# Right operands of the w_mo product: prepared ahead and kept in DRAM, instead of summed and split where they are used

## The chip, the cores and the metric

One core of a Trainium2 chip runs the whole program. The metric is device time in microseconds. Engines: TensorE (PE) multiplies, VectorE (DVE), ScalarE (ACT) and GpSimd (POOL) work on elements, and the sync queue (SP) issues nearly all transfers.

## The reference

One decoder layer on 1024 tokens of width 1024, in float32:

```python
x = x + hybrid_mixer(rmsnorm(x, norm_mix), w_in, ..., w_out)
x = x + memory_attention(rmsnorm(x, norm_mem), rmsnorm(mem, norm_memkv), w_mq, w_mkv, w_mo)
x = x + conv_ffn(rmsnorm(x, norm_ffn), w_up, conv_w, conv_b, w_down)
return rmsnorm(x, norm_final)
```

The mixer has one input projection, three kinds of attention (differential, dilated, and one that keeps the top 256 keys of each query) and an output projection. `memory_attention` is `softmax(q k^T / 16) v` over 256 memory tokens in four heads, with `q = h @ w_mq`, and its result `o` of 1024 x 1024 goes through `o @ w_mo`, which is the product that the change concerns.

## The kernel before, in words

**Precision.** Every float32 matrix is split in a high part (a copy by ScalarE to the type fp32r) and a low part (the source minus the high part, by VectorE or GpSimd). `mm3` (L182) multiplies high by high, high by low and low by high: three matmuls of 128 x 128 by 128 x 512 for one step.

**Strassen products.** The products with w_out (`prod_a`), w_mq (`prod_b`) and w_mo (`prod_d`, L1931) are of 1024 x 1024 by 1024 x 1024, done with seven products of half size in place of eight (`class Product`, L1390). Each of the seven, called n, has four chunks c of 128 along the inner dimension; such a pair is a unit, and it has an order x, from 0 to 83 (56 to 83 for `prod_d`). A unit needs one left and one right operand of 128 x 512, each a pair of high and low. Where the method wants a sum, it is made first, in place of one of the raw blocks (`left_of`, `right_of` L1374, `operand` L1385): the right operands of n = 1, 2 and 3 are raw blocks of w_mo, those of 5, 6, 7 and 4 are sums, 16 units in all. A unit of `prod_d` takes two of eight slots, so it begins when the unit four before it has been multiplied. Product 4, the last, walks over its four chunks twice, each time for two of the four row blocks. In `prod_d` the left operands come from the attention's output Q, the right ones from w_mo, loaded raw into two tiles `wraw` by `load_weights` (L1623) when `prod_b` has all its operands (`tiles_d` L1901), and `needs_d` (L1923) makes units wait for these loads.

**Order of the work.** The order of the instructions on PE, ACT and DVE (and POOL in the second part) is fixed before the program is built, by a model: `class Flow` runs generators that yield an engine, a cost and a rank, and each modelled engine takes the lowest rank in its queue. Engines and the sync queue then carry their instructions out in the order of emission, each waiting for its own data. `ready` (L105) chooses between DVE and POOL for operations that may go to either (`either`, L1313), by the longer of the engine's queue and the queue of a shared port, plus the cost; `issue` (L117) makes such an operation wait until the port is free. There are two flows: the mixer (`build_mixer`, L304) and everything up to the first eight products of the up-projection. In the mixer the attention's items have ranks 0 to 63, the evacuations of the projections -1, the projections on PE 100, and the top-k search 200 or, when it is late, -4.

**After the product.** The sums of `prod_d` are added to the rows of the residual stream (`x1rows`). Rows 0 to 3 (of eight blocks of 128) are complete after product 3, the fifth of the order 1, 5, 6, 2, 3, 7, 4. `normed_rows` (L1531) squares them on ACT, takes the root on DVE in twelve small steps, and scales them on DVE (`xn<-x1rows`, rank 83.2 for rows 0 to 3, 82 for the others); `turned_rows` (L1555) transposes them on PE into the tiles h3T. From these the up-projection's operands T1 to T7 are made (`half_operand` L2353, `tokens` L2386): T1 and T2 are splits of rows 0 to 3, the others hold sums that include rows 4 to 7. The up-projection begins with two products that need T1 and T2 for each of two weight columns, and then needs T7. The T tiles take the places of `prod_d`'s operands and rows; the tiles of h3T, T7 and T3 are counted in `tp_s`.

Of the kernel before, what the change touches and what calls it, by code (L numbers as in the profile page):

```python
# [14 lines left out]
F32 = mybir.dt.float32  # L15
F32R = mybir.dt.float32r
# [5 lines left out]
OP = mybir.AluOpType  # L22
AX = mybir.AxisListType

P = 128
# [24 lines left out]
class Gate:  # L50
    def __init__(self):
        self.open, self.waiting = False, []
# [7 lines left out]
class Flow:  # L60
# [3 lines left out]


    def __init__(self):
        self.t, self.events, self.count = 0.0, [], 0
        self.queue = {e: [] for e in (PE, ACT, DVE, POOL, DMA)}
        self.free = {e: True for e in self.queue}
        self.load = dict.fromkeys(self.queue, 0.0)  # L70
        self.port, self.port_load = 0.0, 0.0
# [33 lines left out]
    def ready(self, s, op):  # L105
        self.count += 1
        if isinstance(op[0], tuple):
            e = min(op[0], key=lambda e: max(self.load[e], self.port_load) + op[1][e])
            op = (e, op[1][e], partial(op[2], e), op[3], True)
        self.load[op[0]] += op[1]  # L110
        if len(op) > 4:
            self.port_load += op[1]
        rank = op[3] if len(op) > 3 else s[1]
        heapq.heappush(self.queue[op[0]], (rank, self.count, s, op))
        self.issue(op[0])

    def issue(self, e):  # L117
        if self.free[e] and self.queue[e]:
            _, _, s, op = heapq.heappop(self.queue[e])
            op[2]()  # L120
# [39 lines left out]
def trunk(ctx, tc, a, out):  # L160
# [98 lines left out]
    memk_d = [dram.tile([P, KC, MEM], F32, name=f"memk_{s}") for s in range(2)]  # L259
    memv_d = [dram.tile([P, 2, D], F32, name=f"memv_{s}") for s in range(2)]  # L260

    def gload(pool, g, tag, **kw):
# [24 lines left out]
    SMALL = 0.15  # L287
    SETUP = 26.0
    WARM = 1
    COLD = 6.0  # L290
# [13 lines left out]
    def build_mixer():  # L304
# [945 lines left out]
        def load_mixed(half, u):  # L1250
            yield mixed[u, half]
            yield from move(0.73, load(mix[half][:, u], mix_d[u][half]))

        where_w = {f"iq{c}": 3072 + P * c for c in range(4)}
        for u, cs in enumerate(units):
# [19 lines left out]
        go(late_pieces(), 80)  # L1275
        go(out_weights(), 90)
        with tc.manual_schedule(engines=engines):
            flow.run()
# [34 lines left out]
    def either(n, f, rank):  # L1313
        return (DVE, POOL), {DVE: t_dve(n), POOL: t_pool(n)}, f, rank

# [74 lines left out]
    class Product:  # L1390
# [14 lines left out]
        def unit(self, n, c):  # L1405
# [11 lines left out]
            a = go(operand(sa, x, *left_of(n, lambda i, j: self.A(i, j, c))), x)  # L1417
            b = go(operand(sb, x, *right_of(n, lambda i, j: self.B(i, j, c), self.last)), x)
            yield a
# [196 lines left out]

    h2, wm, wo2 = {}, {}, {}
    h2_in, h2_hit = after_each([(l, q) for l in range(2) for q in range(2)], 4)
    wm_in = {(j, i): Gate() for j in range(2) for i in range(2)}
    wo2_in = {(j, i): Gate() for j in range(2) for i in range(2)}  # L1620
    h2_new = {l: Gate() for l in range(2)}
# [279 lines left out]
    def tiles_d():  # L1901
        yield from all_made(prod_b, 7, 4)
        for j in range(2):
            go(load_weights(a["w_mo"][0], wo2, wo2_in, j, 56), 56)
        for _ in range(2):
            put(tp_s)
# [16 lines left out]
    def needs_d(n, c):  # L1923
        return {
            1: (o_done[c, 0], wo2_in[0, c // 2]),
            5: (o_done[c, 1], o_done[4 + c, 1]),
            6: (wo2_in[1, c // 2],),
            2: (o_done[4 + c, 0],),
        }.get(n, ())
# [4 lines left out]
        lambda i, j, c: Q[4 * j + c][:, i],  # L1934
        lambda i, j, c: wo2[i][:, c, 512 * j : 512 * j + 512],
        needs_d,
# [18 lines left out]
    def xn_slots():  # L1955
# [4 lines left out]
        for _ in range(4):  # L1960
            put(x_s)
        for _ in range(2):
            put(tp_s)

# [727 lines left out]
```

## Time and profile before

| | us |
|---|---|
| time, median of 3 runs (lowest, highest) | 1650.21 (1649.19, 1655.34) |
| the profiled execution, its own time | 1653.56 |
| its span, first to last instruction | 1651.8 |
| PE busy | 1591.3 |
| DVE busy | 1432.7 |
| ACT busy | 922.7 |
| POOL busy | 469.0 |

The stages follow each other in the trace: the mixer to about 667 us, the product with w_out, the product with w_mq from about 753, the memory attention from about 800, the product with w_mo up to 976, the up-projection from 992 to about 1424, and the down-projection. A busy time counts an instruction from its start to its end, so neighbours on a pipelined engine overlap; the starts tell the pace.

### The profile page before, as it was taken

The page shows a single profiled execution, that of the slowest core. Times are in us where ns is not written, and L with a number is a line of the kernel's source. Part 1 is how long each engine was busy: PE and PEld are TensorE (multiplying, and loading weights), DVE is VectorE, ACT ScalarE, POOL GpSimd, SP SyncE. Part 2 cuts the span into 40 slices and gives each one's busy share as a digit, 9 for nine tenths or more (in the row PEclk, how much of TensorE's full clock was granted, in tenths as well). Part 3 has the DMA queues.
Part 4 walks back from the last instruction along what each step waited for, and adds up shares of the span by engine and source line. Part 5 has one row for each costly group of instructions (what it writes and reads, how often), then busy time and mean ns, then how long its engine had stood idle before and what let it go on. Part 6 is the DMA issues. An engine that isn't in the chain of part 4 may idle for free.

```text
span 1651.8 us, 23507 instructions
## 1 busy us (share of the span) xinstructions
PE 1591.3 (96%) x7853; PEld 1319.2 (80%) x7853; DVE 1432.7 (87%) x2721; ACT 922.7 (56%) x1753; POOL 469.0 (28%) x541
## 2 busy tenths in 40 slices
PE   7989999999999999999999988999999999999997
PEld 7778888888888877878888866888888888887885
DVE  7557999999899987899988999898788888889986
ACT  5345688699865466646655455444444444453443
POOL 3311333232321103010111103342223232436672
PEclk9999999999999999999999999999999999999998
DMA  8484344523434464524052121222222221986532
GB/s 292 121 258 119 96 102 110 125 80 102 123 85 107 122 217 160 197 105 153 1 191 77 52 102 51 73 89 82 89 89 91 77 77 52 324 296 214 185 128 102
DMA packets 162619, 211.25 MB, mean 128 GB/s; under 512 B 13546, under 2 KB 101954, under 8 KB 162498
## 3 DMA queue, kind: packets, MB, share of 16 engines
q1 hardware_dynamic: 161921, 207.65, 40.2%
q10 hardware_dynamic: 576, 2.10, 0.3%
q8 instruction: 62, 1.02, 0.3%
q14 instruction: 60, 0.48, 0.1%
HBM read 145.16 MB, written 41.74 MB: 113 GB/s over the span
## 4 chain that ended last, share of the span: by engine, by line
PE 68%; DVE 19%; issue 6%; DMA 3%; POOL 2%; ACT 1%; SPq 1%; DVEq 0%; ACTq 0%; POOLq 0%
PE up L183 8%; PE up L184 8%; PE up L185 8%; PE pj L183 5%; PE pj L185 5%; PE pj L184 5%; DVE operands L1317 3%; PE trp L980 2%; DVE s L120 2%; PE pr L184 2%; PE dn L184 2%; PE dn L185 2%; PE pr L185 2%; PE dn L183 2%; PE pr L183 2%
## 5 line engine op out<-in xcount | busy, mean ns | idle before, releaser
L184 PE MATMUL up<-T,wo 128*128 128x512 f32 x616 | 242.3, 393 | 4.2 <-DVE T L1317 4.2
L183 PE MATMUL up<-T,wo 128*128 128x512 f32 x616 | 241.6, 392 | 1.5 <-ACT wo L2013 1.2
L185 PE MATMUL up<-T,wo 128*128 128x512 f32 x616 | 241.8, 393 | 0.0
L2011 POOL TENSOR_TENSOR wst<-wst 128x512 f32<-128x512 f32 x82 | 123.3, 1514 | 306.2 <-DVE wo L2005 253.9
L183 PE MATMUL pj<-h1T,wh 128*128 128x512 f32 (+1 forms) x464 | 189.4, 408 | 0.0
L185 PE MATMUL pj<-h1T,wl 128*128 128x512 f32 (+1 forms) x464 | 182.3, 393 | 0.0
L184 PE MATMUL pj<-h1T,wh 128*128 128x512 f32 (+1 forms) x464 | 182.0, 392 | 0.0
L2013 ACT ACTIVATE wo<-wst 128x512 fp32r<-128x512 f32 x144 | 89.6, 628 | 165.5 <-PE up L185 92.3
L184 PEld LDWEIGHTS up<-T,wo 128*128 128x128 f32 x616 | 116.0, 188 | 31.0 <-DVE T L1317 5.4
L183 PEld LDWEIGHTS up<-T,wo 128*128 128x128 f32 x616 | 116.0, 188 | 28.0 <-ACT wo L2013 1.6
L185 PEld LDWEIGHTS up<-T,wo 128*128 128x128 f32 x616 | 116.1, 188 | 25.8 <-DVE wo L1317 0.4
L183 PE MATMUL pr<-operands 128*128 128x512 f32 x336 | 134.6, 400 | 2.0 <-ACT operands L120 1.8
L184 PE MATMUL pr<-operands 128*128 128x512 f32 x336 | 132.8, 395 | 2.4 <-DVE operands L1317 2.2
L185 PE MATMUL pr<-operands 128*128 128x512 f32 x336 | 132.2, 394 | 2.3 <-DVE operands L1317 2.3
L120 POOL TENSOR_TENSOR wl<-st,wh 128x512 fp32r<-128x512 f32 (+1 forms) x58 | 77.5, 1336 | 192.3 <-ACT wh L120 184.9
L2005 DVE TENSOR_TENSOR wo<-wst,wo 128x512 fp32r<-128x512 f32 x141 | 118.2, 840 | 3.5 <-ACT wo L2013 3.5
L2044 DVE SCALAR_TENSOR_TENSOR ring<-ring,convv 128x1023 f32<-128x1023 f32 (+1 forms) x88 | 116.8, 1329 | 0.0
L120 ACT ACTIVATE s<-s,nm 128x128 f32<-128x128 f32 (+7 forms) x128 | 98.9, 773 | 29.1 <-DVE nm L120 26.9
L184 PE MATMUL dn<-dl,dh 128*128 128x512 f32 x280 | 109.4, 391 | 1.0 <-DVE dl L2236 0.9
L185 PE MATMUL dn<-dh,dl 128*128 128x512 f32 x280 | 109.2, 390 | 0.0
L183 PE MATMUL dn<-dh 128*128 128x512 f32 x280 | 109.0, 389 | 0.0
L185 PEld LDWEIGHTS pj<-h1T,wl 128*128 128x128 f32 (+1 forms) x464 | 86.6, 187 | 20.4
(352 smaller groups left out, 4189.2 us busy)
## 6 DMA issues: line engine op xcount, KB each, us to landing
wst<-in_w_up_dram SPq DMA_DIRECT2D x44, 512.0 KB, 3.8
st<-in_w_in_dram SPq DMA_DIRECT2D x56, 256.0 KB, 2.9
passing<-act SPq DMA_DIRECT2D x48, 256.0 KB, 3.9
act<-ring SPq DMA_DIRECT2D x22, 512.0 KB, 2.6
passing<-in_w_down_dram SPq DMA_DIRECT2D x42, 256.0 KB, 6.6
score<-in_w_mkv_dram SPq DMA_DIRECT2D x32, 256.0 KB, 4.0
kd<-kh SPq DMA_DIRECT2D x64, 128.0 KB, 2.3
kl<-kl SPq DMA_DIRECT2D x64, 128.0 KB, 2.3
```

What stands on the lines that cost most here:

```text
L120: op[2]()
L183: nc.tensor.matmul(ps, lh, rh, start=start, stop=False)
L184: nc.tensor.matmul(ps, lh, rl, start=False, stop=False)
L185: nc.tensor.matmul(ps, ll, rh, start=False, stop=stop)
L980: nc.tensor.transpose(tr[:, j * P : (j + 1) * P], s[x][:, kb * P : (kb + 1) * P], ident)
L1317: return either(n, lambda e: engine[e].tensor_tensor(out, x, y, op), rank)
L2005: eng.tensor_tensor(s[:, 1], src, s[:, 0].bitcast(F32), OP.subtract)
L2011: e.tensor_tensor(src, a, b, op)
L2013: nc.scalar.activation(s[:, 0], src, AF.Copy)
L2044: f()
```

## The change

A new generator `prepare` in the mixer, beginning at 46 us of the model's time, makes the 28 right operands of `prod_d`: in each step it loads a block of w_mo (128 x 512), makes the sum if there is one (DVE or POOL), copies the high part (ACT), makes the low part (DVE or POOL) and stores both in DRAM, all with rank 60. `prod_d` then loads each right operand ready, high and low in one transfer of 512 KB. The loads of raw w_mo, their gates and their two tiles go; the two tiles are counted free for h3T and T at once. In the model, an operation that needs the port now names the engines for which it does, and an engine whose first operation would wait for the port for more than 0.1 us takes the best one that doesn't need it.

```diff
     def ready(self, s, op):
         self.count += 1
         if isinstance(op[0], tuple):
-            e = min(op[0], key=lambda e: max(self.load[e], self.port_load) + op[1][e])
-            op = (e, op[1][e], partial(op[2], e), op[3], True)
+            e = min(op[0], key=lambda e: max(self.load[e], self.port_load if e in op[4] else 0.0) + op[1][e])
+            op = (e, op[1][e], partial(op[2], e), op[3]) + ((True,) if e in op[4] else ())
...
     def issue(self, e):
         if self.free[e] and self.queue[e]:
-            _, _, s, op = heapq.heappop(self.queue[e])
+            q = self.queue[e]
+            free = [x for x in q if len(x[3]) < 5] if self.port > self.t + 0.1 and len(q[0][3]) > 4 else []
+            _, _, s, op = x = min(free or q[:1], key=lambda x: x[:2])
+            q.remove(x)
+            heapq.heapify(q)
...
+    wmo_d = {(n, c): dram.tile([P, 2, 512], F32, name=f"wmo_{n}_{c}") for n in range(1, 8) for c in range(4)}
...
+    PREPARE = 46.0
...
+        def prepare():
+
+            yield PREPARE
+            x, y = (ip.tile([P, 512], F32, name=f"prep{i}") for i in "xy")
+            high, low = ip.tile([P, 512], F32R, name="preph"), y.bitcast(F32R)
+            both = lambda n: ((DVE, POOL), {DVE: dve(n), POOL: pool(n)})
+            eng = lambda e: nc.vector if e == DVE else nc.gpsimd
+            for c in range(4):
+                for n, dst, (i, j), diff in (
+                    (1, x, (0, 0), None), (5, y, (0, 1), (y, x)), (6, y, (1, 1), (y, x)), (4, y, (1, 0), (y, x)),
+                    (2, x, (1, 0), None), (3, x, (1, 1), None), (7, y, (0, 1), (x, y)),
+                ):
+                    r = (4 * i + c) * P
+                    yield from move(0.73, load(dst, a["w_mo"][0][r : r + P, 512 * j : 512 * j + 512]), rank=60)
+                    if diff:
+                        yield *both(512), lambda e, diff=diff: eng(e).tensor_tensor(x, *diff, OP.subtract), 60, (DVE, POOL)
+                    yield ACT, act(512, 1), partial(nc.scalar.activation, high, x, AF.Copy), 60
+                    yield *both(512), lambda e: eng(e).tensor_tensor(low, x, high.bitcast(F32), OP.subtract), 60, (DVE, POOL)
+                    yield from move(1.46, copy(wmo_d[n, c][:, 0], high), copy(wmo_d[n, c][:, 1], low), rank=60)
+                    yield 1.0
...
+        go(prepare(), 60)
...
     def either(n, f, rank):
-        return (DVE, POOL), {DVE: t_dve(n), POOL: t_pool(n)}, f, rank
+        return (DVE, POOL), {DVE: t_dve(n), POOL: t_pool(n)}, f, rank, (DVE, POOL)
...
-            b = go(operand(sb, x, *right_of(n, lambda i, j: self.B(i, j, c), self.last)), x)
+            if self.B is None:
+                b = go(moved(1.46, partial(rdma, sb, wmo_d[n, c])), x)
+            else:
+                b = go(operand(sb, x, *right_of(n, lambda i, j: self.B(i, j, c), self.last)), x)
...
     def tiles_d():
         yield from all_made(prod_b, 7, 4)
-        for j in range(2):
-            go(load_weights(a["w_mo"][0], wo2, wo2_in, j, 56), 56)
-        for _ in range(2):
+        for _ in range(4):
             put(tp_s)
...
-            1: (o_done[c, 0], wo2_in[0, c // 2]),
+            1: (o_done[c, 0],),
             5: (o_done[c, 1], o_done[4 + c, 1]),
-            6: (wo2_in[1, c // 2],),
...
-        lambda i, j, c: wo2[i][:, c, 512 * j : 512 * j + 512],
+        None,
...
         yield from all_made(prod_d, 4)
         for _ in range(4):
             put(x_s)
-        for _ in range(2):
-            put(tp_s)
```

## Rows read from the trace of the kernel before

**Rows 1.** Page, busy us (share of the span) xinstructions of each engine.

```profile
PE 1591.3 (96%) x7853; PEld 1319.2 (80%) x7853; DVE 1432.7 (87%) x2721; ACT 922.7 (56%) x1753; POOL 469.0 (28%) x541
```

**Rows 2.** Windows: length; busy PE, PEld, DVE, ACT, POOL (xinstructions); clock; DMA share; GB/s.

```profile
46.00:165.00 119.00, 110.48 (x537) 88.60 (x534) 71.40 (x120) 57.47 (x117) 21.69 (x19) 0.97 0.57 164
165.00:413.00 248.00, 246.65 (x1338) 208.95 (x1337) 236.84 (x711) 200.22 (x486) 81.51 (x224) 1.00 0.41 103
...
845.00:949.80 104.80, 103.46 (x537) 88.17 (x536) 89.53 (x161) 57.13 (x124) 11.85 (x8) 1.00 0.25 83
...
964.00:976.70 12.70, 10.06 (x36) 7.64 (x36) 10.54 (x28) 3.46 (x6) 1.84 (x1) 0.87 0.20 83
976.70:992.20 15.50, 10.58 (x64) 7.95 (x64) 15.08 (x50) 11.30 (x21) 0.00 (x0) 0.89 0.17 69
992.20:1003.00 10.80, 6.57 (x21) 4.55 (x22) 10.48 (x14) 9.97 (x17) 0.00 (x0) 0.89 0.37 98
1003.00:1024.00 21.00, 20.99 (x88) 16.48 (x87) 20.30 (x22) 9.41 (x14) 7.28 (x1) 0.97 0.00 1
```

**Rows 3.** Instructions on `wraw`, 840 to 980 us; durations min/median/max ns.

```profile
L120 ACT ACTIVATE operands<-wraw x28: 614/632/637, 848.0 to 966.6; 128x512 fp32r<-128x512 f32 x28
L1317 DVE TENSOR_TENSOR operands<-wraw,operands x27: 677/687/694, 850.3 to 967.7; 128x512 fp32r<-128x512 f32 x27
L1317 DVE TENSOR_TENSOR wraw<-wraw x15: 679/686/695, 879.7 to 965.8; 128x512 f32<-128x512 f32 x15
```

**Rows 4.** Timeline of TensorE: start, us, line, operation, count [idle before, releaser].

```profile
964.87 0.50 PE L183 MATMUL pr<-operands 128*128 128x512 f32 x1 [0.91 <-ACT operands L120]
967.11 0.79 PE L184 MATMUL pr<-operands 128*128 128x512 f32 x1 [1.74 <-DVE operands L1317]
...
970.82 0.39 PE L185 MATMUL pr<-operands 128*128 128x512 f32 x1
...
976.28 0.39 PE L185 MATMUL pr<-operands 128*128 128x512 f32 x1
...
985.86 1.06 PE L1564 MATMUL trr<-ident,xn 128*128 128x128 f32 x8 [0.71 <-DVE ry L120]
...
992.22 0.51 PE L183 MATMUL up<-T,wo 128*128 128x512 f32 x1 [0.35 <-ACT T L120]
...
1000.91 0.79 PE L184 MATMUL up<-T,wo 128*128 128x512 f32 x1 [3.95 <-DVE T L1317]
```

**Rows 5.** Timeline of VectorE, the same columns.

```profile
961.01 2.49 DVE L120 TENSOR_TENSOR v<-pr,v 128x512 f32<-128x512 f32 x4
963.40 0.69 DVE L1317 TENSOR_TENSOR wraw<-wraw 128x512 f32<-128x512 f32 x1
964.00 0.70 DVE L1317 TENSOR_TENSOR operands<-q,operands 128x512 fp32r<-128x512 f32 x1
...
976.64 1.28 DVE L120 SCALAR_TENSOR_TENSOR xn<-x1rows,ry,gb 128x1024 f32<-128x1024 f32 x1
...
989.27 2.50 DVE L1317 TENSOR_TENSOR wst<-wst 128x512 f32<-128x512 f32 x4
...
1004.38 4.63 DVE L2005 TENSOR_TENSOR T<-h3T,T 128x1536 fp32r<-128x1536 f32 x4
```

**Rows 6.** GpSimd's groups by form, 165 to 413 us: busy us, mean ns.

```profile
L120 POOL TENSOR_TENSOR wl<-st,wh 128x512 fp32r<-128x512 f32 x28 | 37.5, 1341 | 34.9 <-ACT wh L120 32.5 <-PE pss L724 2.4
```

**Rows 7.** Waits of TensorE, 46 to 125 us: total us, times, longest.

```profile
PE psi L723 <- DMA qs<-ql: 4.0, 2, 2.5
```

**Rows 8.** Page, DMA issues: count, KB each, us to landing.

```profile
wst<-in_w_up_dram SPq DMA_DIRECT2D x44, 512.0 KB, 3.8
st<-in_w_in_dram SPq DMA_DIRECT2D x56, 256.0 KB, 2.9
```

**Rows 9.** DMA issues from 845 to 960 us, the same columns.

```profile
x1rows<-x SPq DMA_DIRECT2D x8, 512.0 KB, 6.3
```

**Rows 10.** Windows of 10 us in the mixer, columns as in rows 2.

```profile
90.00:100.00 10.00, 7.49 (x33) 5.98 (x32) 4.30 (x7) 3.58 (x8) 1.30 (x1) 0.98 1.05 325
```

More of the change, by code (lines that the diff above doesn't have):

```diff
@@ L1614, in trunk @@
     )
-    h2, wm, wo2 = {}, {}, {}
+    h2, wm = {}, {}
     h2_in, h2_hit = after_each([(l, q) for l in range(2) for q in range(2)], 4)
     wm_in = {(j, i): Gate() for j in range(2) for i in range(2)}
-    wo2_in = {(j, i): Gate() for j in range(2) for i in range(2)}
     h2_new = {l: Gate() for l in range(2)}
```

## Prediction, made before the changed kernel ran

> **What bounds the kernel now.** I read the page first: TensorE is busy for 96% of the span, VectorE for 87% [rows 1]. So only a place where TensorE stands still, or runs at the lower clock, can give time back. Next I read the table of stretches and looked for such places near the code that the change touches [rows 2]. The reader should see three things in it. From 46 to 165 us TensorE has 8.5 us idle and VectorE, ScalarE and GpSimd have 47.6, 61.5 and 97.3 us. From 165 to 413 us TensorE misses 1.4 us and VectorE 11.2 us of 248, so there the mixer is full, while GpSimd still has 166 us. And between 964 and 1003 us TensorE loses 2.6, 4.9 and 4.2 us, at a granted clock of 0.87 to 0.89, while VectorE is full: 45.9 of 47.3 us from 976.7 to 1024.
>
> The third place is the end of the product with w_mo and the passage to the up-projection, and the timeline says who is late there. TensorE waits 0.91 us and 1.74 us for a w_mo operand's high and low part, then the last matmul starts at 976.28 and the first of the up-projection at 992.22; its second product stalls until 1000.91 for VectorE's low part of T [rows 4]. On VectorE the sum for a right operand of the last product starts only at 963.40, behind the four sums of product 7, and the first normalised row starts at 976.64, although its rows were complete when product 3 had been added [rows 5]. VectorE is the late one, and it is late because of the queue in front of these instructions.
>
> **What the change removes there.** In the product with w_mo it takes away 28 ScalarE copies (632 ns), 27 VectorE subtractions and 15 VectorE sums, with one of each on GpSimd [rows 3]. Back to back, VectorE starts one every 0.60 us (963.40 to 964.00) [rows 5], so 42 x 0.60 = 25 us of VectorE and some 17 us of ScalarE go, spread over 848 to 968 us. Four loads of 1 MB go too; 28 loads of 512 KB come.
>
> *Before 949.8.* TensorE misses 1.3 us of 104.8 there [rows 2]; between 0 and that can come back. I take 1.0.
>
> *964 to 1024.* This stretch takes 60.0 us. What TensorE must do in it at the higher clock: matmuls start every 0.2275 us (24 from 970.82 to 976.28), and 36 of product 4 remain at 964: 8.2 us. 64 transposes, eight in 1.06 us of which the last takes 0.27, so 0.113 each: 7.2 us. The first product of the up-projection and one matmul more, 13 x 0.2275 = 3.0 us, then 23.1 us without a stall from 1000.91 to 1024 [rows 4]. Together 41.5 us, so at most 18.5 us can be won.
>
> What is left of the waits is my choice. (a) The units of product 4 get their slots from product 7, chunk by chunk, and product 4 goes over its chunks in pairs of row blocks, so its chunk 3 is asked for when product 7 ends and needed 3 x 6 x 0.2275 = 4.1 us later. A 512 KB transfer lands 3.8 us after its issue [rows 8], 6.3 us when eight of them are sent together [rows 9]. Waiting ends between 0 and 2.5 us; I take 1.0, since nothing large is sent beside it. (b) With VectorE freed, the four normalised rows 0 to 3 can be done during product 4, and the four sums for the first up operands (989.27) as well [rows 5]; their transposes then lie inside product 4. T1 and T2 still need a tile that prod_d's operands or rows hold until then, and four copies and subtractions. I take 1.5 us. (c) T7 comes last. VectorE must still do, from about 974 us on, four sums (2.4), the small steps of three roots (3), rows 4 to 7 (4.8), the subtractions of T1 and T2 (4.8), two token sums (4.5) and T7 (2.3): 21.8 us, so 996; before, T7's low parts ran from 1004.38 to 1009 [rows 5]. TensorE has 10.9 us of products and 3.6 us of transposes to do from 976.5, so it waits some 4 us. That leaves 6.5 us of waiting: 18.5 - 6.5 = **12 us gained**. Ends: 6 us, if (b) and (c) are no better than half, and 16.
>
> **What it adds in the mixer.** 28 steps, each a load of 256 KB, a ScalarE copy (0.62), a subtraction, two stores of 256 KB, and in 16 of them a sum first. One step lasts about 2.9 us to land [rows 8], 0.63, 1.34 on GpSimd [rows 6], again 2.9 for the stores, 1.0 pause and, in 16 of 28, another 1.34: 9.5 us, an estimate from these rows. So some 12 steps run before 165 us, where the idle time above covers their 19 sums and subtractions (11 us on VectorE or 25 on GpSimd) and 8 us of ScalarE. The other 16 run in the full stretch with 25 such operations: 15 us on VectorE against 11 us idle, or 34 us on GpSimd against 166. The planner compares the queue of each engine plus the operation, so where VectorE has a queue it picks GpSimd. At rank 60 they stand behind nearly all attention work, ahead only of the top-k search when that is on time. I cost the engines at nothing; if that cover is gone, 25 x 0.60 = 15 us of attention work moves towards the mixer's end.
>
> What isn't covered is waiting in order. The planner lets the reader of a load follow 0.73 + 0.9 = 1.6 us behind it, the trace has 2.9 [rows 8], so ScalarE, VectorE or GpSimd can stand 1.3 us per step in front of everything behind it: 0 to 36 us for 28 steps. The sync queue gets 84 issues more, each ahead of a load or a copy of the attention. The nearest row is TensorE's wait for copied queries in this stretch, 4.0 us in two waits [rows 7], with 10 us of 16 full transfer engines (share 1.05) near it [rows 10]. Below nothing: a newly laid out list can also close part of the 8.5 us idle. Ends: 3 us gained, 36 lost. I take **3 us lost**, nearest to that row, since engines other than TensorE have slack in the first half of the steps.
>
> **Traffic.** The change moves 7.3 MB of loads and 14.7 MB of stores into the mixer, and 14.7 MB instead of 4.2 into the product. In the product that is 512 KB per 12 matmuls (2.7 us), while the transfer engines are busy for 0.25 of the time at 83 GB/s [rows 2] and carry 325 GB/s when full [rows 10]: 1.6 us of 2.7. I cost it at nothing beyond (a).
>
> **The other edits.** The new port rule lets a list take work without the port when the port is held. GpSimd has 8 instructions from 845 to 949.8 [rows 2], so the rule has few occasions: nothing, within 1 us either way. Two tiles more are free for h3 and T early; T waits for its source anyway: nothing.
>
> **Sum.** -12 - 1 + 3 = -10 us. The profiled execution took 1653.56 us (span 1651.8 and 1.8 around it), 3.4 above the median of 1650.21; against the median the sum gives **1640 us**.
>
> **Rivals.** *B, only half the tail.* Product 4 still waits for its last transfer, the T tiles come free only at its end, and rows 4 to 7 end late anyhow, so the chain behind them sets the end. For it: T7 and the parts after it hang on rows that product 4 completes. Against it: VectorE is full, so the queue is real. -6 - 1 + 3: 1646.
> *C, a queue that only moves.* The ranks may leave the normalised rows behind product 4's work even with VectorE free, so the gap of 16 us stays and only the stall of 2.6 us goes. Against it: VectorE ran out of such work even now, 10.54 us busy of the 12.7 before 976.7 [rows 2]. -2.6 - 1 + 3: 1649.
> *D, slower: waits in the mixer.* Every step's first reader stands at the head of its engine until the load lands. If TensorE loses the whole 1.3 us in all 28 steps, the mixer costs 36 us and the time is 1650 - 13 + 36 = 1673; at 0.8 us per step, 22 us, it is 1659. It decides from 13/28 = 0.46 us per step on. For it: the full stretch and the narrow margin. Against it: the view of rows 7 has no wait of TensorE for a load of w_in, which the same lists lay out, and GpSimd, which should get most of the sums, has few others behind it.
> *E, transfers as the bound.* 32.5 MB more, at the 325 GB/s of [rows 10], are 100 us if none of it lies beside other work: 1740. Against it: the engines are busy for 0.57 of the time at most in the stretches of [rows 2] up to 413 us and 0.25 in the product, so nearly all of it has room.
> The Trainium skill, page "SBUF — State Buffer", section "A bandwidth-pool intuition that's wrong (but worth ruling out)", says that HBM is almost always the bottleneck end to end, which speaks for E; the shares in this trace do not agree with it.
>
> **How the numbers follow.** About 0.5% (8.25 us) is what a measurement here can tell from no change: 1642.0 and 1658.5 are the bounds. Forecast 0.53, spread 1634 to 1646 by its ends; B 0.27; C 0.10; D 0.08; E 0.02. Three quarters of the forecast lie under 1642 and a fifth of B: faster 0.45. D and E lie above 1658.5: slower 0.10. The rest, 0.45, is within. The range 1632 to 1655 takes in the forecast's ends, B and C, and leaves out D, E and the extreme of the tail.
>
> **What would show it.** Right: no w_mo split in the product, VectorE with about 25 us less busy time from 845 to 976; the first normalised row ahead of product 4's end; a gap of 3 to 6 us, not 16, before the first up product; prepared operands before 350 us, mostly on GpSimd. The forecast is wrong if the first up product still comes 12 us or more behind the last of w_mo, or if the mixer ends over 8 us later, with TensorE waiting behind ScalarE or VectorE instructions that wait for a transfer.

## The result, and the profile after

The changed kernel takes **1670.16 us** (median of 4 runs, 1666.67 to 1673.41) beside 1651.24 for the kernel before on the same chip: ratio **1.0106, 95% interval 1.0079 to 1.0134**. It is slower by 1.1%, where the prediction had 1640 us and a range up to 1655. The profiled execution took 1672.66 us, 2.5 above its median.

The windows of the changed kernel, columns as in [rows 2]; the last five are the product with w_mo, its end, and the passage, some 14 to 22 us later than before.

```profile
46.00:165.00 119.00, 106.19 (x515) 84.14 (x514) 75.34 (x125) 57.45 (x118) 22.04 (x19) 0.97 0.72 221
165.00:413.00 248.00, 237.71 (x1259) 196.79 (x1258) 234.87 (x659) 192.86 (x461) 105.27 (x223) 1.00 0.55 154
866.00:971.50 105.50, 105.50 (x548) 90.23 (x547) 75.13 (x140) 46.52 (x108) 9.81 (x7) 1.00 0.59 190
985.70:998.40 12.70, 11.86 (x63) 9.27 (x62) 12.60 (x30) 5.00 (x10) 0.00 (x0) 1.00 0.38 153
998.40:1006.10 7.70, 4.34 (x28) 3.45 (x27) 7.55 (x30) 7.50 (x15) 0.00 (x0) 0.85 0.33 136
1006.10:1016.90 10.80, 10.80 (x47) 8.66 (x46) 9.78 (x21) 6.37 (x12) 0.00 (x0) 0.79 0.01 2
1016.90:1042.00 25.10, 21.55 (x81) 16.57 (x79) 21.54 (x24) 13.79 (x19) 4.41 (x1) 0.86 0.22 63
```

Beside [rows 2] the reader sees two kernels in one. In the product TensorE now misses nothing (105.50 of 105.50 us; it missed 1.3 of 104.8). In the mixer TensorE is idle for 10.3 us of the stretch from 165 to 413 us, where it was idle for 1.4, and for 12.8 from 46 to 165, where it was 8.5. VectorE, nearly as full as before (234.87 us), has 659 instructions behind it where it had 711: each takes longer, or other ones are being done.

Five marks of the two traces divide the difference: the first matmul of the product with w_out (the mixer's end), the first sum of product 7 on VectorE (961.01 in [rows 5]), the first matmul of the up-projection, the first use of its result, and the end of the span.

| mark, us | before | after | after - before |
|---|---|---|---|
| first matmul of the product with w_out | 670.2 | 695.3 | +25.1 |
| product 7 taken from PSUM | 961.01 | 981.82 | +20.8 |
| first up matmul | 992.2 | 1006.1 | +13.9 |
| first `ring<-up,ta` | 1024.4 | 1042.4 | +18.0 |
| span | 1651.8 | 1670.8 | +19.0 |

So the mixer loses 25.1 us, the products win 4.3, the passage to the first up matmul wins 6.9 more, and the start of the up-projection gives 4.1 back.

The preparation's instructions, in the view of the tile `prepx` (durations min/median/max in ns, first and last start in us; the last line is the time from a load's issue to its landing):

```profile
L125 ACT ACTIVATE preph<-prepx x28: 613/630/644, 63.1 to 430.0; 128x512 fp32r<-128x512 f32 x28
L1278 POOL TENSOR_TENSOR prepy<-prepx,preph x15: 1277/1295/1381, 199.6 to 430.7; 128x512 fp32r<-128x512 f32 x15
L1278 DVE TENSOR_TENSOR prepy<-prepx,preph x13: 670/682/693, 64.5 to 310.7; 128x512 fp32r<-128x512 f32 x13
...
L1276 POOL TENSOR_TENSOR prepx<-prepy,prepx x7: 1288/1290/1386, 186.4 to 376.5; 128x512 f32<-128x512 f32 x7
L1276 DVE TENSOR_TENSOR prepx<-prepy,prepx x5: 693/693/1743, 72.1 to 170.6; 128x512 f32<-128x512 f32 x5
L1276 DVE TENSOR_TENSOR prepx<-prepx,prepy x2: 679/685/691, 133.1 to 221.0; 128x512 f32<-128x512 f32 x2
L1276 POOL TENSOR_TENSOR prepx<-prepx,prepy x2: 1295/1296/1298, 318.4 to 423.6; 128x512 f32<-128x512 f32 x2
...
DMA to landing us min/median/max: 3.4/4.2/5.0
```

A step takes 13.6 us, not 9.5, so 9 of the 28 begin before 165 us, not 12. Of the 44 sums and subtractions 24 went to GpSimd and 20 to VectorE.

What TensorE waits for from 165 to 440 us, first before, then after (total us, times, longest):

```profile
PE av L1011 <- DVE ptl L120: 0.6, 1, 0.6
PE pss L723 <- DVE nm L120: 0.6, 1, 0.6
```

```profile
PE pss L730 <- DVE nm L125: 4.1, 4, 2.1
PE av L1018 <- DVE ptl L125: 3.3, 7, 1.1
PE trp L987 <- DVE s L125: 1.5, 3, 0.9
```

VectorE is late there, with no transfer in TensorE's list. Between 46 and 165 us it is the queries' copies again, as in [rows 7]. Two other lists of that stretch show what stands in order in front of such work: the sync queue is held at the stores until ScalarE has made the high part, and VectorE at the first reader of a step's load. Which of the two makes the copies late is not shown.

```profile
PE psi L730 <- DMA qs<-ql: 7.7, 4, 2.8
```

```profile
SPq L172 <- ACT preph L125: 13.0, 5, 4.8
```

```profile
DVE prepx L1276 <- DMA prepy<-in_w_mo_dram: 7.2, 5, 3.5
```

The passage, on TensorE and on VectorE, as in [rows 4] and [rows 5]:

```profile
988.88 0.47 PE L188 MATMUL pr<-operands 128*128 128x512 f32 x1 [0.84 <-DMA operands<-wmo]
...
993.85 0.63 PE L1596 MATMUL trr<-ident,xn 128*128 128x128 f32 x4
...
1006.14 0.78 PE L188 MATMUL up<-T,wo 128*128 128x512 f32 x1
...
1023.10 0.51 PE L188 MATMUL up<-T,wo 128*128 128x512 f32 x1 [1.79 <-ACT T L2193]
...
1024.93 0.80 PE L189 MATMUL up<-T,wo 128*128 128x512 f32 x1 [1.32 <-DVE T L2031]
```

```profile
992.42 2.48 DVE L125 SCALAR_TENSOR_TENSOR xn<-x1rows,ry,gb 128x1024 f32<-128x1024 f32 x2
...
998.41 0.69 DVE L125 TENSOR_TENSOR x1rows<-pr,x1rows 128x512 f32<-128x512 f32 x1
...
1003.21 0.69 DVE L1346 TENSOR_TENSOR T<-h3T,T 128x512 fp32r<-128x512 f32 x1
...
1011.63 1.76 DVE L2190 TENSOR_TENSOR h3T<-h3T,h3T 128x1536 f32<-128x1536 f32 x1 [0.98 <-ACT h3T L125]
1013.31 1.28 DVE L125 SCALAR_TENSOR_TENSOR xn<-x1rows,ry,gb 128x1024 f32<-128x1024 f32 x1
```

The first normalised rows (992.42) and their transposes (993.85) now lie inside product 4, which ends at 998.2; the wait for the last operand's transfer is 0.84 us. The first up matmul comes 8 us behind the product, not 16. But the last row block is normalised 14.9 us behind the product's last sum (998.41 to 1013.31; before 10.3, 977.83 to 988.1), since many of the small steps of its root stand behind a subtraction of T of 0.69 us (1003.21), and at the end a sum of h3T that waits itself (1011.63) stands in front of it. T7 stalls TensorE at 1023.10 and 1024.93.

### The profile page after: what moved, and what is told of

Its sections match the earlier page's. It is cut to its first block, busy times and chain, and to the rows that moved or that the text cites. A ratio compares the mean times of both kernels' runs of the same rounds, so it can differ in the third digit from the quotient of the medians.

```text
span 1670.8 us, 23756 instructions
## 1 busy us (share of the span) xinstructions
PE 1599.3 (96%) x7850; PEld 1321.1 (79%) x7857; DVE 1429.7 (86%) x2700; ACT 920.4 (55%) x1753; POOL 493.0 (30%) x562
## 4 chain that ended last, share of the span: by engine, by line
PE 63%; DVE 23%; DMA 4%; ACT 3%; issue 3%; POOL 2%; SPq 1%; DVEq 0%; POOLq 0%; ACTq 0%
PE up L189 8%; PE up L190 8%; PE up L188 8%; DVE score L125 3%; PE pr L189 3%; PE pr L190 3%; PE pr L188 3%; PE pj L188 3%; DVE s L125 3%; PE pj L189 3%; PE pj L190 3%; PE dn L190 2%; PE dn L189 2%; PE dn L188 2%; PE trp L987 2%
## 5 line engine op out<-in xcount | busy, mean ns | idle before, releaser
L2037 POOL TENSOR_TENSOR wst<-wst 128x512 f32<-128x512 f32 x82 | 119.4, 1466 | 332.6 <-DVE wo L2031 255.3
```

The lines of the kernel that those rows point to most:

```text
L2037: e.tensor_tensor(src, a, b, op)
```

## Experiments

Unless said otherwise each edit is to the changed kernel, ratios are to the kernel before on the same chip, and "mixer's end" is the first matmul of the product with w_out in the profiled run (670.2 before, 695.3 after). Three theories stood at the start: **H**, engines stand in order until a step's load has landed (rival D of the prediction); **T**, the traffic and the issues on the sync queue; **L**, work added to full engines.

| run | median us | ratio (95%) | mixer's end |
|---|---|---|---|
| e1 no preparation | 1643.31 | 0.9945 (0.9926 to 0.9964) | 670.0 |
| e2 transfers only | 1649.55 | 0.9984 (0.9970 to 0.9998) | 674.1 |
| e3 engines only | 1666.51 | 1.0088 (1.0065 to 1.0111) | 691.2 |
| e4 later readers | 1669.83 | 1.0109 (1.0080 to 1.0138) | 690.1 |
| e5 GpSimd only | 1667.58 | 1.0095 (1.0068 to 1.0122) | 687.6 |
| e6 VectorE only | 1670.50 | 1.0113 (1.0090 to 1.0137) | 693.7 |
| e7 copies only | 1655.09 | 1.0023 (1.0006 to 1.0039) | 679.1 |
| e8 sums, no copies | 1671.13 | 1.0125 (1.0100 to 1.0150) | 689.8 |
| e9 plan without work | 1655.10 | 1.0012 (0.9997 to 1.0028) | 677.0 |
| e10 work without plan | 1661.78 | 1.0065 (1.0047 to 1.0084) | 682.5 |
| e11 nudge | 1647.34 | 0.9968 (0.9955 to 0.9980) | 673.4 |
| e12 port rule alone | 1649.31 | 0.9977 (0.9967 to 0.9987) | 667.2 |
| e13 unplanned, VectorE | 1654.13 | 1.0017 (1.0006 to 1.0029) | 681.8 |
| e14 unplanned, GpSimd | 1662.92 | 1.0071 (1.0058 to 1.0085) | 687.5 |
| e15 unplanned, copies | 1647.39 | 0.9973 (0.9961 to 0.9985) | 672.1 |
| e16 two products | 1661.14 | 1.0062 (1.0044 to 1.0080) | 683.4 |
| e17 list of the change | 1649.73 | 0.9984 (0.9972 to 0.9996) | 671.6 |
| e18 list and transfers | 1653.55 | 1.0010 (0.9996 to 1.0023) | 676.3 |

**Which half, and transfers or engines.** Four kernels:

```diff
e1 -        go(prepare(), 60)
   -partial(rdma, sb, wmo_d[n, c])
   +partial(rdma, sb, memn_d[n % 2][:, c % 2 * 4 : c % 2 * 4 + 4].rearrange(...))
e2 -yield *both(512), lambda e, ...: eng(e).tensor_tensor(x, *diff, OP.subtract), 60, (DVE, POOL)
   +yield 1.2 if diff else 0.0
   (likewise the copy: yield 0.7; the subtraction: yield 1.0)
e3 -yield from move(0.73, load(dst, a["w_mo"]...), rank=60)
   +yield 3.3
   (likewise the stores: yield 4.0; operands as in e1)
e4 +yield 2.0   (behind the load)
   +yield 1.5   (behind the stores)
```

> The preparation in the mixer is left out; the product with w_mo still loads each right operand ready, 512 KB in one transfer, but from another array in DRAM of the same size, so its values are not those of w_mo. This leaves the change's second half alone. The changed kernel begins the product with w_out at 695.0 us against 670.0 before (25 us lost in the mixer) and ends 18 us late, so by the traces the second half gains 7 us. Every theory: the mixer ends at 670 again, within 2 us. If the gain is the one seen, 7 us: 1644. If the forecast's 13 us are there and were hidden by the mixer's new order: 1638.

> The preparation keeps its 28 loads and 56 stores at the same pace, but its sums, copies and subtractions are left out (fixed pauses stand for them), so what is stored is not the operands. Theory H (an engine in order stands still until the step's load, or the step's instruction on another engine, has come): the transfers alone hold nobody, the mixer ends 2 to 8 us late, time 1646 to 1652. Rival T (traffic and the sync queue's 84 issues delay the mixer's own transfers): 20 to 25 us of the 25 remain, 1664 to 1670. Rival L (the added work on full engines): 0 to 3 us, 1644 to 1647.

> The preparation keeps its 44 sums and subtractions and 28 copies, on tiles filled once, with pauses in place of its loads and stores; the product with w_mo loads its right operands from another array, so the values are wrong. Rival L (engine work in a full stretch): 17 to 25 us of the mixer's 25 remain, 1661 to 1669. Theory H: what is left is the waiting between the three engines of a step, 4 to 10 us, 1648 to 1654. Rival T: 0 to 3 us, 1644 to 1647.

> Nothing is left out: in the planner each load of the preparation is followed by 2.0 us more before its reader may be placed, and the stores by 1.5 us more, so that the placed order matches the landing seen in the trace (loads 3.4 to 5.0 us). Theory H: most of the standing still goes, the mixer ends 5 to 12 us late instead of 25, 1650 to 1657. Rivals T and L: no gain, 1666 to 1674.

e1 gains 0.55%, 9 us: the second half of the change does what it was for, together with the port rule, which e1 keeps. e2 gives 6 of them back, e3 24. With no load to wait for, e3 loses nearly what the whole change loses. In e4 the waits of VectorE and ScalarE for a step's load, 7.2 and 1.0 us in the change, are gone (what still waits is GpSimd, 22.1 us where it was 5.4), and it is no faster than the change. So H falls as the main cause, T has some 6 us, and L holds, though all four kernels also have other lists.

**Which engine.** e3 again, with the 44 sums and subtractions on one engine, without them, or without the copies:

```diff
e5 -yield *both(512), lambda e: eng(e).tensor_tensor(low, ...), 60, (DVE, POOL)
   +yield POOL, pool(512), lambda: nc.gpsimd.tensor_tensor(low, ...), 60, True
e6 +yield DVE, dve(512), lambda: nc.vector.tensor_tensor(low, ...), 60, True
e7 (sums and subtractions) +yield 1.2 if diff else 0.0, +yield 1.0
e8 (copies) +yield 0.7
```

> As e3_engines_only (loads and stores of the preparation are left out; the operands of the product come from another array, so the output is not the reference's), but all 16 sums and 28 subtractions go to GpSimd, none to VectorE: 44 x 1.3 us on GpSimd, 28 x 0.63 us on ScalarE. Without any of them the first product with w_out came at 670.0 us, with the planner's mixture (20 on VectorE, 24 on GpSimd) at 691.2. Theory V (VectorE's time: the mixer is full on VectorE between 165 and 440 us, and what is put there is added): no more than 5 us left, first product at 670 to 676, ratio 0.995 to 0.998. Theory P (a conflict between the two: while GpSimd runs one of these, VectorE's operations with two inputs in SBUF take longer or wait): as much or more than the mixture, first product at 690 to 705, ratio 1.008 to 1.017. Theory A (the ScalarE copies): as e3, 691.

> As e3_engines_only (same parts left out), but all 16 sums and 28 subtractions go to VectorE: 44 x 0.60 = 26 us. Theory V: those that run between 165 and 440 us are added to a full engine, some 30 x 0.6 = 18 us, and the rest find room: first product at 685 to 697, ratio 1.004 to 1.012. Theory P: nothing is added on GpSimd, so only VectorE's own time, and the planner does less of the top-k search there: 674 to 684, ratio 0.997 to 1.004. Theory A: as e3, 691.

> As e3_engines_only, and the sums and subtractions are left out too (pauses of 1.2 and 1.0 us in the list in their place): what stays is 28 ScalarE copies of 0.63 us. ScalarE has 26 us free of 135 from 165 to 300 us and 22 of 140 from 300 to 440, so theories V and P expect first product at 670 to 674, ratio 0.994 to 0.997. Theory A (the copies stand in the way of the softmax's exponentials, on which TensorE waits): 685 to 692, ratio 1.003 to 1.009.

> As e3_engines_only, and the 28 ScalarE copies are left out (a pause of 0.7 us in the list in their place): 44 sums and subtractions on VectorE or GpSimd as the planner chooses. Theories V and P: as e3, first product at 686 to 693, ratio 1.005 to 1.010. Theory A: 670 to 676, ratio 0.995 to 0.998. In between would mean that the three engines' parts add up.

None of the theories fits all four. Wherever the sums and subtractions go, the mixer ends 18 to 24 us later than in e1, and even the copies alone, which have room on ScalarE, lose 9. Each of these kernels has other lists, for the planner lays out the mixer anew around whatever it books. That had to be taken apart first.

**List or work.** In e9 the planner books e3's work and nothing is emitted for it; in e10 it is emitted and the planner books no time for it, so that all the mixer's other instructions keep e1's order; e11 books 0.3 us on three engines at 200 us and emits nothing; e12 is the kernel before with the port rule.

```diff
e9  -partial(nc.scalar.activation, high, x, AF.Copy)
    +lambda: None
    (likewise sums and subtractions; on e3)
e10 -yield ACT, act(512, 1), partial(nc.scalar.activation, high, x, AF.Copy), 60
    +yield ACT, 0.0, partial(nc.scalar.activation, high, x, AF.Copy), 60
    +yield act(512, 1)
    (likewise sums and subtractions; on e3)
e11 +yield 200.0
    +for e in (ACT, DVE, POOL):
    +    yield e, 0.3, lambda: None, -20
e12 the changes of ready, issue and either, on the kernel before
```

> The plan of e3_engines_only with none of its work: the planner books the same 28 ScalarE copies, 28 subtractions and 16 sums at the same times on the same engines, but nothing is emitted for them, so TensorE's order is that of e3_engines_only and nothing is prepared (operands from another array, output not the reference's). The first product with w_out came at 670.0 us without the preparation and at 691.2 in e3. Theory W (work: the added instructions take their engines' time, or stretch VectorE's by GpSimd's): 670 to 674, ratio 0.994 to 0.997. Theory R (re-laid lists: booking 72 operations changes which of the attention's instructions stand ahead of which, and the new order fits the chip's real times worse): 685 to 692, ratio 1.004 to 1.009. In between would divide the 21 us.

> The work of e3_engines_only without its plan: the same 28 copies, 28 subtractions and 16 sums (20 on VectorE, 24 on GpSimd, the same engine for each) are emitted, but the planner books them at no time, so the order of all other instructions on TensorE is that of e1_no_prepare (operands from another array, output not the reference's). Theory W: 688 to 695, ratio 1.006 to 1.012, since every added instruction still delays what is behind it. Theory R: 670 to 676, ratio 0.995 to 0.998.

> e1_no_prepare with the planner nudged: at 200 us of its time it books 0.3 us on ScalarE, VectorE and GpSimd each, and nothing is emitted for them; the order of some 1200 of TensorE's 7374 instructions changes, and no work is added (operands from another array, output not the reference's). Theory W: within 3 us of e1: first product at 668 to 673, ratio 0.993 to 0.997. Theory R, in its strong form (any re-laying costs, because the lists of the kernel before happen to fit): 676 or later, ratio 0.998 or more.

> The kernel before with the new port rule alone (an operation of a list may pass one that waits for the port); nothing is prepared, the product with w_mo splits its own operands. The prediction put this edit at nothing within 1 us: ratio 0.999 to 1.001. If part of the 8 us that e1_no_prepare gained were the port rule's, 0.995 to 0.998; if the rule hurts, above 1.002.

Both theories hold in part. Against e1, booking alone costs 0.67% (11 us; 7 by the mixer's end), the work alone 1.2% (20 us), and both together, e3, 1.43%. A nudge of the planner costs 4 us, with intervals that just overlap. e12 is faster than both kernels. Its mixer has the list of before, instruction for instruction, so the edit's own part is what lies behind it: the way from the product's end to the first up matmul is 14.3 us (973.3 to 987.6) instead of 15.9 [rows 4], and from product 7's sums to the first `ring<-up,ta` it is 60.8 instead of 63.4. The 3 us by which its mixer ended earlier are not the edit's: from 46 to 165 us its granted clock was 1.00, where it was 0.97 in [rows 2] (1.00 is 2.4 GHz, the upper of its two levels).

```profile
46.00:165.00 119.00, 112.03 (x556) 89.54 (x555) 74.82 (x127) 59.91 (x122) 22.78 (x20) 1.00 0.59 167
```

This result lies in the bounds that were named for the case that part of e1's gain is the port rule's. How much of e1's 9 us that is, no run shows: none has the second half without the rule.

**Which engine, with the order held.** e10 with all 44 on VectorE, all on GpSimd, and the copies alone. The fourth kernel leaves nothing out: it has the port rule and prepares only the operands of products 7 and 4.

```diff
e13, e14 (on e10) -picks = iter("pdddddddddddddpdpppdpdpppdppppdppppppppppppd")
                  +picks = iter("ddd...")     (44 times d; e14: 44 times p)
e15 (sums and subtractions) +yield 1.2 if diff else 0.0, +yield 1.0
e16 on e12: prepare without its step for n = 2, and
    +if n not in (4, 7):
    +    continue
    in Product.unit
    +if x >= 56 and n in (4, 7):
    +    b = go(moved(1.46, partial(rdma, sb, wmo_d[n, c])), x)
```

> As e10_work_without_plan (order of e1_no_prepare on TensorE, work not booked by the planner, loads and stores of the preparation left out, operands from another array, so the output is not the reference's), with all 44 sums and subtractions on VectorE. Theory P (VectorE's instructions that read two tiles in SBUF stand while GpSimd runs an added operation: 11.6 us of the 18 us that e10 lost from 165 to 440 us): no added GpSimd operation, so VectorE's other instructions keep their durations within 2 us in all; what is lost is VectorE's own time in the full stretch, some 28 of the 44 operations x 0.69 = 19 us less the 15 us that it is idle there: first product at 674 to 686. Theory V (VectorE's time is what counts, wherever it comes from): 690 or later, since twice as many operations as in e10 lie on it.

> As e13_unplanned_vector, with all 44 on GpSimd and none on VectorE. Theory P: VectorE's own instructions get longer by 44 x 0.46 = 20 us at most (e10: 11.6 us by 25 operations), some of it before 165 us where there is room: their sum between 60 and 445 us is 12 to 20 us above that of e1_no_prepare, and the first product comes at 682 to 690. Theory V: nothing is added on VectorE: durations as in e1 within 2 us, first product at 670 to 674.

> As e13_unplanned_vector, with the sums and subtractions left out too: only the 28 ScalarE copies of 0.63 us, in the order of e1_no_prepare. Theories P and V: ScalarE has 20 us and more free in each of the two full stretches, so first product at 669 to 673, ratio 0.994 to 0.997; then the 9 us that e7_copies_only lost were the planner's re-laying. If ScalarE's copies themselves stand in the way of the exponentials: 676 or later.

> A version of the whole kernel, nothing left out: the new port rule, and only the right operands of products 7 and 4 of the product with w_mo prepared in the mixer (24 loads, 16 sums, 8 copies, 8 subtractions, 16 stores instead of 28, 16, 28, 28 and 56), at the start, where VectorE and ScalarE have room; the other five split theirs in the product as before. Theory P: with some 10 of its operations behind 165 us the mixer loses 2 to 6 us (and re-laying gives or takes some 4), the tail gains 3 to 5: 1645 to 1653, ratio 0.996 to 1.001. If any preparation in the mixer costs as the whole one does: 1655 to 1662.

Here the same instructions stand in the same order, so VectorE's can be compared one by one. Its groups from 165 to 440 us (busy us, mean ns of one), in e1, e13 and e14:

```profile
L125 DVE TENSOR_SCALAR_CACHE_REDUCE score<-mask,sel_thr_d 128x384 int16<-128x384 int16 (+1 forms) x68 | 54.2, 804 | 2.2 <-POOL sel_thr_d L125 2.0
...
L125 DVE SCALAR_TENSOR_TENSOR s<-s,r,s 128x128 f32<-128x128 f32 (+7 forms) x32 | 26.4, 826 | 0.1
L125 DVE SCALAR_TENSOR_TENSOR score<-rl,iw,score 128x512 f32<-128x512 f32 (+2 forms) x10 | 7.2, 734 | 0.0
```

```profile
L125 DVE SCALAR_TENSOR_TENSOR s<-s,r,s 128x128 f32<-128x128 f32 (+7 forms) x32 | 27.3, 853 | 0.1
```

```profile
L125 DVE TENSOR_SCALAR_CACHE_REDUCE score<-mask,sel_thr_d 128x384 int16<-128x384 int16 (+1 forms) x68 | 54.1, 803 | 1.9 <-POOL sel_thr_d L125 1.7
L125 DVE SCALAR_TENSOR_TENSOR s<-s,r,s 128x128 f32<-128x128 f32 (+7 forms) x32 | 31.2, 977 | 0.1
...
L125 DVE SCALAR_TENSOR_TENSOR score<-rl,iw,score 128x512 f32<-128x512 f32 (+2 forms) x10 | 9.3, 941 | 0.0
```

With all the work on GpSimd, two large groups of VectorE's instructions that read two tiles in SBUF take 18 and 28% longer (977 against 826 ns, 941 against 734), and the group with a single tile as input is not touched (803 against 804). Over all the 903 instructions of VectorE from 60 to 445 us that stand in both traces, the durations sum to 20.5 us more in e14 than in e1, and those that overlap a GpSimd instruction to 23.0 more; in e13, with no added GpSimd work, they sum to 1.4 less; in e10, with 25 operations on GpSimd, to 11.6 more. In e14 it is few instructions that pay: 27 of the 903 are longer by over 0.25 us, 23.9 us in all. One of them, four elements wide, first in e1, then in e14 with GpSimd's added subtraction that covers it:

```profile
214.53 0.16 DVE L125 SCALAR_TENSOR_TENSOR rz<-rz,rv 128x4 f32<-128x4 f32 x1
```

```profile
217.88 1.22 DVE L125 SCALAR_TENSOR_TENSOR rz<-rz,rv 128x4 f32<-128x4 f32 x1
```

```profile
217.78 1.30 POOL L125 TENSOR_TENSOR prepy<-prepx,preph 128x512 fp32r<-128x512 f32 x1
```

This is what the Trainium skill, page "SBUF — State Buffer", section "🔬 SBUF: two separate sides", states: VectorE and GpSimd share a pair of ports, an exclusive lock that is held for a whole instruction, and a VectorE instruction with two SBUF inputs and a GpSimd instruction that reads SBUF shut each other out. The traces agree, on GpSimd's side too: its 28 subtractions take 1.43 us on average in e14, with a median of 1.30 and a longest of 2.32.

How far VectorE's list falls behind e1's from 165 us to the mixer's end then reads 4.4 us for the copies alone (e15), 11.2 with 44 operations on VectorE (e13), 16.0 with 44 on GpSimd (e14), 17.4 with the mixture (e10); the mark at 165 us makes them uncertain by some 2 us. So the engine that was free, GpSimd, is the dearer one. VectorE's busy time alone doesn't say why: over its instructions from 165 to 440 us it grows by 16.4 us in e13 and by 12.9 in e14, but its idle time falls by 5.4 us in e13 and rises by 3.3 in e14. So added operations fill part of VectorE's gaps here, and longer instructions do not; why was not tried.

e16's miss: the forecast had no price for the list and the transfers at the start, where TensorE is busy for 105.8 us of 119 (112.0 in e12) and waits 7.3 us for the queries' copies. Its mixer ends 16.2 us behind e12's (in this stretch its clock was 0.97 beside e12's 1.00), and the whole is 0.85% slower than e12. How that loss divides between list, transfers and work wasn't tried.

**The change's own list.** The last two keep the order of all its other instructions:

```diff
e17 -yield from move(0.73, load(dst, a["w_mo"]...), rank=60)
    +yield from move(0.73, lambda: None, rank=60)
    (likewise stores, copies, sums and subtractions; operands as in e1)
e18 (copies, sums and subtractions only) +lambda: None
```

> The change's own plan with nothing of the preparation emitted: no loads, no copies, no sums or subtractions, no stores; all other instructions in the change's order (the product reads another array, so the output is not the reference's). The first product with w_out comes at 695.3 us in the change and at 670.0 without the preparation. If the earlier parts add up (7 for the list, 14 for the engines' work, 4 for the transfers): 675 to 679, ratio 0.998 to 1.002. If the list itself is the larger part: 683 or later. If it is nothing: 670 to 672.

> The change's own plan with the loads and stores of the preparation emitted and none of its copies, sums and subtractions (two tiles are set to constants once; the output is not the reference's). Parts that add up: 679 to 684, ratio 1.000 to 1.005, and the change's other 12 to 16 us are the engines' work. Transfers that wait for one another behind the sync queue: 687 or later.

By their ratios both came within the bounds in which the parts add up. By the mixer's end both came earlier, and e17's 671.6 us lies where the list was to be nothing. Against e1 the list costs 0.39% (6 us), the transfers 0.26% more (4 us), the engines' work 0.96% more (1.0106 - 1.0010: 16 us); each figure is good to about 3 us. Of the list's 6 us only 1.6 are in the mixer, where the order is another; the rest lies behind it, where e17 has e1's instructions, at a lower mean granted clock over the whole run (0.987 over its ten runs, 0.990 over e1's four). So in the mixer the new list is nearly free.

In the same order, VectorE's instructions from 60 to 445 us sum to 9.5 us more in the change than in e18, and to 13.9 more where they overlap GpSimd; from 165 to 440 us TensorE's list falls back by 9.5 us. So past 165 us the loss is about what VectorE's own instructions are longer.

Before 165 us the change loses another 9.5 us against e18. Of these, 2.6 stand there at 60 us, before the first copy of the preparation (63.1), so they are not the work's. The other 6.9 are lost between 60 and 165 us. TensorE waits 7.7 us for the queries' copies there, and in e18 2.1:

```profile
PE psi L730 <- DMA qs<-ql: 2.1, 4, 0.7
```

Behind one of these waits, 2.1 us at 142.1, the change's clock was 0.50 from 143.6 to 147.0 us; in e18 it was 1.00 from 46 to 165. Two things in this stretch come only with the work and the transfers together, which neither e3 nor e18 has: stores wait for ScalarE, and VectorE waits for loads. No run divides the 6.9 us between them, the queries' copies and the clock.

## Why the prediction was wrong

**The step that failed** is "I cost the engines at nothing; if that cover is gone, 25 x 0.60 = 15 us of attention work moves towards the mixer's end", in the part on the mixer. The engines' work costs 16 us. The clause that names what happens without cover was about right in size, by luck as to its cause, and it stood in no term of the sum and in no rival. Past 165 us the cover failed for another reason than I considered: GpSimd had its 166 free microseconds, took 24 of the 44 operations, all of them past 165 us, and took VectorE's time with them: 9.5 us. Before 165 us, where the idle time was to cover 19 operations and 8 us of ScalarE, some 7 us more were lost among the sync queue's stores, VectorE's waits for loads and the queries' copies; which of these it was stays open.

**The 3 us** for waits and transfers, taken between 3 gained and 36 lost, are 4 for the transfers without the work (e18). The list alone costs 6 by the times, of which 1.6 are in the mixer; it had no term, and the sum allowed for a new list only as a gain.

**The product, before 949.8 us**: 1.0 forecast; 4.3 in the change, 3.4 in e1 (from the first matmul of the product with w_out to product 7's sums, 290.8 us before, 286.5 and 287.4).

**The tail**: 12 forecast; from product 7's sums to the first `ring<-up,ta` 63.4 us became 60.6 in the change and 58.6 in e1, 2.8 and 4.8 gained. (a) was right: 0.84 us for the transfer. (b) was right in its first half: rows 0 to 3 and 28 transposes lie in or just behind product 4. (c) is mis-sized: the 21.8 us of VectorE's list were counted by their busy time, and the roots of rows 4 to 7 are chains, many steps of which stand behind one of T1's and T2's subtractions; the last block is 14.9 us behind the product instead of 10.3. In the change the first up products also ran at a granted clock of 0.79 (0.92 in e1). Lost time returned as a later stall, and the net of the second half is 8 to 9 us with the port rule's part, not 13. Two small slips of the sum itself: 974 + 21.8 is 995.8, and TensorE's 10.9 and 3.6 us from 976.5 end at 991.0, so (c) was 4.8 us and not 4; and the upper end of (a) is 6.3 - 4.1 = 2.2 us, not 2.5. The port rule, put at nothing within 1 us, gave the kernel before 3.8 us by the times and 2.6 in the passage (e12).

**Rivals.** For the tail, B's 6 us is nearest to e1's 4.8 and C's 2.6 to the change's 2.8. D had the sign, and its 1659 to 1673 hold the time, but its mechanism is not the main one: e4 takes the wait for the load off VectorE and ScalarE and gains nothing, and e3 has no load and loses nearly as much. What is left of D lies before 165 us, in VectorE's 7.2 us at loads and the sync queue's 13.0 at stores. E falls: the mixer's loads and stores cost 4 us. C falls: the gap went from 16 to 8 us.

**What was to show it**: VectorE's relief came (75.13 us busy in 105.5 before product 7's sums, 89.53 in the like stretch of [rows 2]; to the product's end 97.99 from 866 to 998.4, 114.26 from 845 to 976.7, so 16 us where 25 were named, with the four normalised rows now inside), and so did the early rows; the gap is 8 us where 3 to 6 were named. The sign against the forecast came too, a mixer over 8 us later; the waits for transfers behind which I looked for it are there before 165 us, and past it only for 0.3 us on ScalarE.

## What to carry to other kernels

A free engine is no cover for work when it shares a port with the full one: where GpSimd has room and VectorE has none, price each GpSimd operation that reads SBUF by what it adds to VectorE (here 20.5 us for 44 operations, 0.47 us each, against 0.60 to 0.69 for doing one on VectorE itself, of which its idle time takes a part). In a mixer whose lists a planner lays out, hold the order and change the work, or hold the work and change the order; kernels in which both move (e2 to e8) show only their sum. Here the port rule alone (e12, 0.23% faster than before) is the version to keep, and the preparation is worth nothing as long as it costs 27 us where the second half, with the port rule, gains 9.

## What the runs showed of the hardware

The exclusion goes both ways and reaches small instructions: `rz<-rz,rv`, 128 x 4 elements, took 228 ns in e1 and 403 in e14 on average, and the single one shown above 1.22 us instead of 0.16. Not every one is hit: `ry<-rz,ry`, of the same size and the next step of the root, took 201 and 206.

TensorE's clock from 46 to 165 us, where it is idle for some 8 of 119 us, was granted at 0.97 in some runs and at 1.00 in others, with the same list (0.97 before, 1.00 in e12), and the mixer's end moved by 3 us. Before, it was at 0.51 from 51.7 to 55.2 us, behind a wait of 3.0 us, and again from 99.5 to 103, behind one of 2.5; in e12 the longest wait of the stretch was 1.7 us and the clock did not fall. At 165 us e12 was 4.3 us ahead. A profile of one run can't settle a difference of that size in this kernel.
